# High parts of plain weight tiles written by rounding DMAs from HBM, without raw tiles

## The chip, the cores and the metric

The kernel runs on one core of a Trainium2 chip. The metric is the device time of one execution in microseconds (us), taken as the median of several runs. Beside the times there is one profiled execution with a trace of every instruction and DMA.

## The reference

One step of a streaming encoder with one layer. A prompt of 512 tokens and a sample of 64 tokens (with states and caches from earlier chunks) pass through the same weights: a mixer (gated DeltaNet beside gated linear attention), cross-attention into 256 memory tokens, and a ConvFFN, each behind an RMSNorm and with a residual. All numbers are float32.

```
def _mixer(h, p, l, conv_prev, s_a, s_b):
    proj = h @ p['w_in'][l]
    qkv, b_raw, a_raw, z_a, q_b, k_b, v_b, g_lr, z_b, gt_a, gt_b = _split_cols(proj, IN_SIZES)
    ...
    merged = jax.nn.sigmoid(gt_a) * y_a + jax.nn.sigmoid(gt_b) * y_b
    return merged @ p['w_o'][l], conv_new, s_a_new, s_b_new

def _conv_ffn(h, w_up, conv_w, conv_b, w_down, prev):
    u, new = _causal_dwconv(h @ w_up, conv_w, prev)
    u = u + conv_b
    gate, val = u[..., :D_FF], u[..., D_FF:]
    return (jax.nn.silu(gate) * val) @ w_down, new

def _trunk(...):
    x = x + _mixer(_rmsnorm(x, ...), ...)
    x = x + _cross_attn(_rmsnorm(x, ...), mem_k, mem_v, w_mq, w_mo)
    x = x + _conv_ffn(_rmsnorm(x, ...), w_up, conv_f_w, conv_f_b, w_down, ffn_prev)
    ...
    return _rmsnorm(x, norm_final), states
```

Outputs are the 576 rows of y, the new states of both attention kinds and both convolutions, and the memory keys and values.

## The kernel before

Tokens lie along the free axis (512 + 64 = 576 columns, in two halves of 288 or 290), channels on the 128 partitions. A weight tile is 128 x 1024: eight blocks of 128 x 128, which a projection (`proj`, `tile_proj`) multiplies with the eight chunks of x into one output chunk in PSUM (`sm`).

TensorE takes float32r operands, so every float32 operand is split in two: a rounded high part h and a low part lo = w - h. A product is then three matmuls: h with the high part of x, h with its low part, lo with its high part. For most weights (the kinds in `SUMMED`, line 177) the projection runs `late`: all matmuls with h first, two thirds of its time, then those with lo. Names in the trace: `w` are split weight tiles, h and lo alike; `wr` raw ones; `xh`, `xl`, `ach`, `acl` split activations; `gt` the mixer's gates; `fu`, `fc`, `fst`, `fout` the tiles of the FFN's convolution; `ws` sums of weights; `wt` and `wd` the weights in HBM, `wd` those of the down-projection, in pieces of 640 to 1024 columns that belong to parts of the 22 FFN chunks.

How a plain weight is made (`emit_weight`, lines 621 to 651): SyncE (SP) issues a load of the raw tile, float32, from HBM. ACT then writes lo = -raw with an ACTIVATE and h = raw with a CAST (`split_summed`). Then GpSimd (POOL) issues an accumulating DMA that reads the same weights from HBM again and adds them to lo. The few weights outside `SUMMED` (mk, mv and one tile of the down-projection) get lo by a subtraction of raw and h on DVE or POOL instead. A second kind of weights, marked "*" in the list `WORDER`, comes in pairs: seven products of sums of their halves take the place of eight (`emit_product`, line 660). They begin in the mixer's output projection and need raw tiles, from which DVE adds the sums `ws`.

Tiles live in rings: `w` with 6 tiles (WB), `raw` with 4 (RAWB), and in the FFN, where the mixer's space is free, 3 more `w` tiles (`wf`) and 1 more raw tile (`rawf`). `w_tile` and `raw_tile` take a tile whose last reader is done first (`Driver.first`). `fetch` (line 733) makes weights ahead in the order of `WORDER` as long as split tiles are left (`room`). From the up-projection on (`LATE0`), the split isn't made at once but some 25 us of the plan ahead of its use (`LEADD`, `defer`).

The first three weights come in halves between the chunks of x at the start (lines 765 to 776): SP alternates x, half a weight, x, half a weight.

All work passes through `Driver` (lines 251 to 509), which replays the program against a table of costs and puts every operation of ACT, DVE, POOL and SP at the place in its engine's order where it would come by the plan. Each engine runs its own instructions strictly in that order and waits at each for its inputs, and so an instruction that waits holds up all behind it. Every recorded operation has the line of the driver's helper, 292, so the views go by tile names.

Of the kernel before, what the change touches and what calls it, by code (L numbers as in the profile page):

```python
# [10 lines left out]
F32 = mybir.dt.float32  # L11
F32R = mybir.dt.float32r
I32 = mybir.dt.int32
AF = mybir.ActivationFunctionType
# [3 lines left out]
P = 128  # L18
D = 1024
# [6 lines left out]
SLOT = 582  # L26
HT = T // 2
NS = 59
RAWB = 4
NBANK = 8  # L30
SPARE = 2
OGO = ("oa", 3)
WB = 6
WF = 3
RF = 1
# [32 lines left out]
def weight_order():  # L68
    seq = list(HEADS)
    for m in range(NPG):  # L70
        seq += [("gta", m), ("gtb", m)]
    seq += [("*", u) for u in product_order(GPAIRS[:NG1], True)]
    seq += [("outb", m) for m in range(NB)]
    seq += [("outa", m) for m in range(NB)] + [("out", m) for m in range(NB, 4)]
    seq += [("*", u) for u in product_order(GPAIRS[NG1:])]
    seq += [("out", m) for m in range(max(NB, 4), 8)]
    for kd, i in ATT:
        if kd == "wo":
            seq += [("*", u) for u in product_order(WPAIRS, True)]
        else:  # L80
            seq += [(kd, 2 * i + j) for j in range(2)]
    seq += [("mo", 0), ("mo", 1)] + [("*", u) for u in product_order(MPAIRS, True)]
    for kd, i in FFN:
        if kd == "up":
            seq += [("up", i), ("up", NJ + i)]
        elif kd == "upx":
            seq.append(("*", (up_pair(i[0]), i[1])))
        elif kd == "dn1":
            seq.append(("dn", i))
        elif kd == "dns":  # L90
            seq += [("*", u) for u in product_order(i)]
        else:
            seq += [("dn", (m, 3)) for m in i]
    return seq
# [3 lines left out]
PARTS = [list(range(0, 5)), list(range(5, 11)), list(range(11, 18)), list(range(18, 22))]  # L98
# [54 lines left out]
WORDER = weight_order()  # L153
# [17 lines left out]
    WPRE.append(WPRE[-1] + weight_cost(w_))  # L171
LEADD, LEADV = 25.0, 18.0
LATE0 = WORDER.index(("up", 0))

# [5 lines left out]
def free(ap):  # L182
    n = 1
    for d in ap.shape[1:]:
        n *= d
    return n
# [64 lines left out]
class Driver:  # L251
# [82 lines left out]
        self.fresh.add(n)  # L334
        return tile_

    def first(self, tag, bufs, other, n):

        free = [(self.swapped if t in ("rawf", "wf") else 0.0) if len(self.ring.get(t, ())) < k else self.free_at(t)[0] for t, k in ((tag, bufs), (other, n))]
        return free[0] < free[1]  # L340

    def idle(self, name, bank=False):
        w, r = (max([0.0] + list(log.get(name, {}).values())) for log in (self.wrote, self.seen))
# [51 lines left out]
    def accumulate(self, out, in_, issuer):  # L395

        issue = self.place("G", self.open([out], []), 1.0)
        cost = self.FIXED["D"] + 2 * free(out) * self.PACE["D"]
        end = self.place("D", issue + 2.0, cost) + cost + 1.0
        self.mark(self.wrote, end, [out])  # L400
        self.put(issue, [(issuer.dma_start, (out, in_), dict(accum_op=ALU.add))])

    def hold(self, fn, cost, args, kw):
        out, ins = args[0], args[1:]
        self.due(self.now)
        t = max(self.ready_at(*ins), self.latest(self.seen, out), self.latest(self.ringed, out)) + HOP
        self.now = max(self.now, t)
        self.put(self.now, [(fn, args, kw)])
        self.now += cost
        self.mark(self.seen, self.now, ins)  # L410
        self.mark(self.wrote, self.now, [out])
        self.last = max(self.last, self.now)
        self.flush(self.now - BACK)
# [99 lines left out]
def tile_trunk(ctx, tc, xT, memT, wt, wd, vec, cst, w0, wgate, st_gdn, st_conv, st_gla, st_ffn, ckT, cv,  # L513
               o_y, o_gdn_p, o_conv, o_gla_p, o_ffn, o_mk, o_mv, o_gdn_s, o_gla_s):
    nc = tc.nc
    drv = PE = Driver(nc.tensor, nc.sync)
    V, A, G = Engine(drv, "V", nc.vector), Engine(drv, "A", nc.scalar), Engine(drv, "G", nc.gpsimd)
    X = Either(V, G)

    DMA, DMO = drv.load, drv.store  # L520
# [4 lines left out]
    wp = ctx.enter_context(tc.tile_pool(name="wp", bufs=2))  # L525
# [5 lines left out]
    fp = None  # L531

    def nm(s):
        cnt[0] += 1
        return f"{s}{cnt[0]}"
# [39 lines left out]
    def f(ap):  # L575
        return ap.bitcast(F32)
# [5 lines left out]
    def keep(t_):  # L582
        drv.pending.add(t_[:].tensor.name)
        return t_

    def drop(*aps):
        for ap in aps:
            drv.pending.discard((ap if hasattr(ap, "tensor") else ap[:]).tensor.name)

    def raw_tile():  # L590
        while all(n in drv.pending for tag in ("raw", "rawf") for n in drv.ring.get(tag, ())) and len(drv.ring.get("raw", ())) == RAWB:
            make(next(iter(unmade)))
        if fp is not None and drv.first("rawf", RF, "raw", RAWB):
            return keep(drv.rotate("rawf", RF, fp.tile([P, 1024], F32, tag="rawf", name=nm("wr"), bufs=RF)))
        return keep(drv.rotate("raw", RAWB, wp.tile([P, 1024], F32, tag="raw", name=nm("wr"), bufs=RAWB)))

    wnames = set()

    def w_tile():
        if fp is not None and drv.first("wf", WF, "w", WB):  # L600
            t_ = drv.rotate("wf", WF, fp.tile([P, 1024], F32R, tag="wf", name=nm("w"), bufs=WF))
        else:
            t_ = drv.rotate("w", WB, wp.tile([P, 1024], F32R, tag="w", name=nm("w"), bufs=WB))
        wnames.add(t_[:].tensor.name)
        return keep(t_)

    unmade = {}

    def make(i):
        fn = unmade.pop(i, None)  # L610
        if fn is not None:
            fn()

    def defer(i, fn, at):
        if i < LATE0:
            fn()
            return
        unmade[i] = fn
        drv.later(at, lambda: make(i))

    def emit_weight(i, at=0.0):
        kind, idx = WORDER[i]
        if kind == "*":
            wready[i] = emit_product(i, at, *idx)
            return
        raw = raw_tile()
        n = 1024
        if kind == "dn":
            m, p = idx
            n = len(PARTS[p]) * 128  # L630
            src = wd[m, :, PART0[p] * 128:PART0[p] * 128 + n]
        elif kind in ("outa", "outb"):
            n, c = 512, 512 * (kind == "outb")
            src = wt[WIDX[("out", idx)], :, c:c + 512]
        else:
            src = wt[WIDX[(kind, idx)]]
        DMA(raw[:, :n], src)
        h = w_tile()
        h, lo = (h[:, 0:512], h[:, 512:1024]) if n <= 512 else (h[:], w_tile()[:])
        summed = kind in SUMMED and (kind, idx) != ("dn", (7, 3))  # L640

        def split_():
            if summed:
                split_summed(h[:, :n], lo[:, :n], raw[:, :n], src)
            else:
                A.copy(h[:, :n], raw[:, :n])
                X.tensor_tensor(lo[:, :n], raw[:, :n], f(h[:, :n]), op=ALU.subtract)
            drop(raw[:])

        defer(i, split_, max(drv.ready_at(raw[:, :n]), at - (LEADD if summed else LEADV)))  # L650
        wready[i] = (h, lo)

    def split_summed(h, lo, raw, src):
        A.activation(lo, raw, AF.Copy, scale=-1.0)
        A.copy(h, raw)
        drv.accumulate(lo, src, nc.gpsimd)
# [3 lines left out]
    def emit_product(i, at, pair, prod):  # L660
# [32 lines left out]
        s1 = lambda: made("s1", lambda: a21, lambda: a22)  # L693
        s2 = lambda: made("s2", s1, lambda: a11)
        w = w_tile()
        h, lo = w[:, 0:n], w[:, 512:512 + n]
        summed = prod in ("P1", "P2", "Q4") or prod == "Q5" and n > 256 and pair[0][0] not in ("wo", "dn")
# [19 lines left out]
    def weight(kind, idx, ahead=True, held=False):  # L717

        i = wpos[0]
        assert WORDER[i] == (kind, idx), (WORDER[i], kind, idx)  # L720
        wpos[0] = i + 1
        for j in [j for j in wready if j < i - held]:
            drop(*wready.pop(j))
        if i not in wready:
            emit_weight(i)
        make(i)
        if ahead:
            fetch(i + 1, i)
        return wready[i]
# [3 lines left out]
    def fetch(i, now=None):  # L733

        now = i if now is None else now
        room = WB + (WF if fp is not None else 0)
        for j in range(i, len(WORDER)):
            if j in wready:
                continue
            if j >= wlimit[0]:  # L740
                break
            kd_, i_ = WORDER[j]
            if len(drv.pending & wnames) + (1 if kd_ in ("*", "outa", "outb") or kd_ == "dn" and len(PARTS[i_[1]]) <= 4 else 2) > room:
                break
            emit_weight(j, drv.now + WPRE[j] - WPRE[now])

# [15 lines left out]
    mbc_t = cp.tile([P, 256], F32, name="mbc")  # L762
    cst_t = small_tile([P, NM - 256], F32, tag="cst", name="cst", bufs=1)
    x = []
    raws = [wp.tile([P, 1024], F32, tag="raw", name=nm("wr"), bufs=RAWB) for _ in range(3)]
    for t_ in raws:
        keep(drv.rotate("raw", RAWB, t_))

    WPART = {k: (n // 2, 512 * (n % 2), 512 * (n % 2) + 512) for n, k in enumerate((0, 1, 2, 3, 5, 6))}
    for k in range(KT):  # L770
# [3 lines left out]
        if k in WPART:  # L774
            i, a, b = WPART[k]
# [294 lines left out]
    def c_heads():  # L1070

        while not drv.ready(OGO):
            yield WAIT
# [1544 lines left out]
```

## Time and profile before

| | |
|---|---|
| median of 3 runs | 1069.32 us (1068.57 to 1070.27) |
| span of the profiled execution | 1067.2 us |
| granted TensorE clock | 1.00 in all stretches |
| DMA packets | 171.33 MB, mean 161 GB/s |
| POOL `w <-` DMA issues waiting for ACT `w` | 407.2 us in 142 waits |
| ACT `w` waiting for PE `sm` (a tile not yet free) | 48.0 us in 43 waits |

The profiled execution is 2.1 us shorter than the median, which holds time outside the span as well. Rows of groups read: line, engine, operation, out<-in, shapes and count, then busy time, mean ns, and the idle time before with what ended it. Time that an engine other than TensorE sits idle costs nothing by itself.

### The profile page before, as it was taken

The numbers are of one execution on the slowest core, as the hardware profiler recorded it, in microseconds if no ns is written. First come the engines' busy times: TensorE is split into PE (matmuls) and PEld (weight loads), VectorE is DVE, ScalarE is ACT, GpSimd is POOL, SyncE is SP. The second block draws the span as 40 slices with busy tenths as digits, with TensorE's granted clock in tenths as the row PEclk, the third lists the DMA queues.
The fourth block names the chain that finished last, engine by engine and source line by source line (L and its number), as shares of the span: only waits on it lengthen the run. The fifth ranks groups of instructions, "written<-read, shape, count | busy, mean of one in ns | idle before, by whom it ended". The sixth has DMA issues, their size and how long they took to land.

```text
span 1067.2 us, 21405 instructions
## 1 busy us (share of the span) xinstructions
PE 1059.6 (99%) x8162; PEld 1045.0 (98%) x8162; DVE 749.7 (70%) x1480; ACT 704.6 (66%) x1410; POOL 356.5 (33%) x581
## 2 busy tenths in 40 slices
PE   9999999999999999999999999999999999999997
PEld 8999999999999999999999999999999999999997
DVE  6666855767675776878647676778877776688665
ACT  7665547555667667456666778767776775777645
POOL 1243216233534233124221235344343333332324
PEclk9999999999999999999999999999999999999999
DMA  9665345353449979588664467858887798878844
GB/s 303 147 142 138 64 121 128 76 123 85 123 76 209 214 162 264 192 226 221 175 165 139 81 166 180 194 111 176 183 191 168 155 218 188 185 159 190 183 90 111
DMA packets 68182, 171.33 MB, mean 161 GB/s; under 512 B 7920, under 2 KB 14576, under 8 KB 68080
## 3 DMA queue, kind: packets, MB, share of 16 engines
q0 software_dynamic: 30672, 71.19, 38.8%
q1 hardware_dynamic: 36976, 98.26, 28.1%
q8 instruction: 64, 1.05, 0.4%
q10 hardware_dynamic: 432, 0.53, 0.1%
q14 instruction: 38, 0.31, 0.1%
HBM read 157.50 MB, written 5.37 MB: 153 GB/s over the span
## 4 chain that ended last, share of the span: by engine, by line
PE 96%; DMA 1%; ACT 1%; issue 0%; DVE 0%; SPq 0%; ACTq 0%
PE sm L292 96%; DMA w<-wt 1%; ACT w L292 1%; DMA wr<-wt 0%; ACT gt L292 0%; DVE w L292 0%; DVE x L292 0%; DVE acl L292 0%; DVE yo L292 0%; ACT ao L292 0%; ACT ach L292 0%; ACT xh L292 0%; DVE xl L292 0%; SPq L292 0%; DVE ws L292 0%
## 5 line engine op out<-in xcount | busy, mean ns | idle before, releaser
L292 PE MATMUL sm<-xh,w 128*128 128x290 f32 (+3 forms) x2304 | 446.7, 300 | 0.2 <-DMA w<-wt 0.2
L292 PEld LDWEIGHTS sm<-xh,w 128*128 128x128 f32 x2304 | 356.7, 189 | 2.2 <-DMA w<-wt 0.4
L292 PE MATMUL sm<-xl,w 128*128 128x290 f32 (+3 forms) x1152 | 269.9, 295 | 0.2 <-DVE xl L292 0.2
L292 POOL DMA_DIRECT2D w<-wt x152 | 135.6, 904 | 339.7 <-ACT w L292 289.0
L292 PE MATMUL sm<-ach,w 128*128 128x288 f32 (+2 forms) x1212 | 231.0, 296 | 0.6 <-ACT gt L292 0.4
L292 PEld LDWEIGHTS sm<-xl,w 128*128 128x128 f32 x1152 | 200.4, 188 | 0.4 <-DVE xl L292 0.4
L292 PEld LDWEIGHTS sm<-ach,w 128*128 128x128 f32 x1212 | 189.7, 188 | 1.2 <-ACT gt L292 0.6
L292 ACT CAST w<-wr 128x512 fp32r<-128x512 f32 (+5 forms) x209 | 159.0, 764 | 18.9 <-PE sm L292 15.4
L292 ACT ACTIVATE w<-wr 128x512 fp32r<-128x512 f32 (+5 forms) x186 | 141.8, 764 | 23.3 <-PE sm L292 20.5
L292 PE MATMUL sm<-acl,w 128*128 128x256 f32 (+2 forms) x606 | 146.8, 295 | 0.2 <-DVE acl L292 0.2
L292 ACT CAST w<-ws 128x512 fp32r<-128x512 f32 (+1 forms) x136 | 80.3, 598 | 49.0 <-DVE ws L292 26.6
L292 PEld LDWEIGHTS sm<-acl,w 128*128 128x128 f32 x606 | 107.4, 188 | 0.5 <-DVE acl L292 0.5
L292 DVE TENSOR_TENSOR w<-ws,w 128x512 fp32r<-128x512 f32 (+1 forms) x108 | 73.5, 688 | 24.9 <-ACT w L292 22.9
L292 DVE SCALAR_TENSOR_TENSOR fc<-fu,vec,fc 128x578 f32<-128x578 f32 x88 | 70.5, 816 | 3.3 <-ACT fc L292 3.3
L292 PE MATMUL sm<-sh,w 128*128 128x290 f32 x288 | 61.2, 297 | 0.0
L292 DVE TENSOR_TENSOR x<-x,sm 128x320 f32<-128x320 f32 (+3 forms) x98 | 40.1, 437 | 22.9 <-PE sm L292 22.6
L292 POOL DMA_DIRECT2D w<-wd x34 | 29.8, 885 | 74.9 <-ACT w L292 65.1
L292 ACT ACTIVATE fc<-fu,vec 128x578 f32<-128x578 f32 x44 | 38.1, 871 | 15.1 <-POOL fu L292 14.8
L292 PEld LDWEIGHTS sm<-sh,w 128*128 128x128 f32 x288 | 47.6, 189 | 0.0
L292 DVE TENSOR_TENSOR ws<-ws,wr 128x512 f32<-128x512 f32 (+1 forms) x67 | 44.5, 664 | 1.1
L292 PE MATMUL sm<-oh,w 128*128 128x256 f32 (+1 forms) x256 | 45.1, 296 | 0.0
L292 PE MATMUL sm<-sl,w 128*128 128x290 f32 x144 | 39.8, 297 | 0.0
(401 smaller groups left out, 1933.4 us busy)
## 6 DMA issues: line engine op xcount, KB each, us to landing
wr<-wt SPq DMA_DIRECT2D x129, 512.0 KB, 5.7
w<-wt POOLq DMA_DIRECT2D x51, 512.0 KB, 7.0
w<-wt POOLq DMA_DIRECT2D x101, 256.0 KB, 6.3
w<-ws POOLq DMA_DIRECT2D x27, 256.0 KB, 5.3
x<-xT SPq DMA_DIRECT2D x16, 288.0 KB, 6.0
wr<-wt SPq DMA_DIRECT2D x14, 256.0 KB, 5.3
wr<-wd SPq DMA_DIRECT2D x8, 448.0 KB, 5.1
w<-wd POOLq DMA_DIRECT2D x8, 448.0 KB, 6.8
```

Source lines behind the costliest of these rows:

```text
L292: fn(*args, **kw)
```

## The change

For plain weights in `SUMMED` there is no raw tile any more. POOL issues a DMA from HBM straight into h, whose type is float32r, so the DMA rounds on its way (`Driver.cast`). ACT writes lo = -h from the rounded tile, and POOL's accumulating DMA adds the weights to it as before. The ACT cast and the SP load are gone. The products, mk, mv and the one tile of the down-projection are made as before. In the first stage, up to four weights before the first product (`EARLY`), the four raw tiles serve as further split tiles: `w_tile(both)` may take them and `fetch` counts them as room, so ten tiles are there instead of six. Which ring a tile comes from is decided by `Driver.sooner`, over as many rings as are offered.

```diff
+EARLY = next(i for i, w in enumerate(WORDER) if w[0] == "*") - 4
+RINGS = dict(w=WB, wf=WF, raw=RAWB, rawf=RF)
...
+    def cast(self, out, in_, issuer):
+
+        issue = self.place("G", self.open([out], []), 1.0)
+        cost = self.FIXED["D"] + free(out) * self.PACE["D"]
+        end = self.place("D", issue + 2.0, cost) + cost + 1.0
+        self.mark(self.wrote, end, [out])
+        self.put(issue, [(issuer.dma_start, (out, in_), {})])
...
+    def w_tile(both=False):
+        t_ = ring_tile(F32R, "w", "wf", *(("raw",) if both else ()))
         wnames.add(t_[:].tensor.name)
...
-        raw = raw_tile()
...
-        DMA(raw[:, :n], src)
-        h = w_tile()
-        h, lo = (h[:, 0:512], h[:, 512:1024]) if n <= 512 else (h[:], w_tile()[:])
         summed = kind in SUMMED and (kind, idx) != ("dn", (7, 3))
+        raw = None if summed else raw_tile()
+        h = w_tile(i < EARLY)
+        h, lo = (h[:, 0:512], h[:, 512:1024]) if n <= 512 else (h[:], w_tile(i < EARLY)[:])
+        if summed:
+            drv.cast(h[:, :n], src, nc.gpsimd)
+        else:
+            DMA(raw[:, :n], src)
 
         def split_():
             if summed:
-                split_summed(h[:, :n], lo[:, :n], raw[:, :n], src)
+                A.activation(lo[:, :n], f(h[:, :n]), AF.Copy, scale=-1.0)
+                drv.accumulate(lo[:, :n], src, nc.gpsimd)
...
-            if len(drv.pending & wnames) + (1 if ...) > room:
+            if len(drv.pending & wnames) + (1 if ...) > room + (RAWB if j < EARLY else 0):
```

By the count of instructions, POOL issues 297 DMAs where it issued 213, SP has 162 rows where it had 246, and ACT 1169 rows where it had 1250. TensorE has 7326 rows in both, with the same matmuls; in the first stage they interleave a little differently.

POOL at the start of the program, before (`w_317<-wt` is an accumulate onto a low part; `rt` and `u` belong to the first norm and the convolution):

```order
8 L292 MEMSET mhalf 128x16
9 L292 DMA w_317<-wt 128x1024
10 L292 MEMSET rin_366 128x8
11 L292 DMA w_320<-wt 128x1024
12 L292 MEMSET u_321 128x3
13 L292 DMA w_326<-wt 128x1024
```

And now; `w_315`, `w_317`, `w_322`, `w_324` and `w_326` are high parts, `w_316`, `w_318` and `w_323` low ones:

```order
8 L294 MEMSET mhalf 128x16
9 L294 DMA w_315<-wt 128x1024
10 L294 DMA w_317<-wt 128x1024
11 L294 DMA w_322<-wt 128x1024
12 L294 DMA w_324<-wt 128x1024
13 L294 DMA w_326<-wt 128x1024
14 L294 MEMSET rin_367 128x8
15 L294 DMA w_316<-wt 128x1024
```

Five rounding DMAs stand ahead of the first accumulate. The first waits for nothing, the second for DVE (a raw tile of the start), the next three for TensorE. On SP the loads of these tiles, which stood behind the constants, are gone.

ACT in the mixer's gates before, at the place of 400 us in the profile (`w_5233`, `w_5271` low parts, `w_5232`, `w_5270` high ones):

```order
471 L292 COPY gt_5229<-sm_5212 128x288
472 L292 ACTIVATE w_5233<-wr_5231 128x1024
473 L292 CAST w_5232<-wr_5231 128x1024
474 L292 COPY gt_5230<-sm_5234 128x288
475 L292 ACTIVATE w_5271<-wr_5269 128x1024
476 L292 CAST w_5270<-wr_5269 128x1024
477 L292 ACTIVATE gt_5088<-gt_5088 128x576
478 L292 ACTIVATE gt_5087<-gt_5087 128x576
```

And now:

```order
437 L294 COPY gt_5155<-sm_5138 128x288
438 L294 ACTIVATE w_5158<-w_5157 128x1024
439 L294 COPY gt_5156<-sm_5159 128x288
440 L294 ACTIVATE gt_5013<-gt_5013 128x576
441 L294 ACTIVATE gt_5014<-gt_5014 128x576
442 L294 COPY gt_5155<-sm_5138 128x288
```

Of four weight operations between the gates' one is left.

POOL in the down-projection between the chunks of the FFN, before (640-wide pieces are the plain weights; `w_9897` and `w_9919` low parts):

```order
379 L292 COPY fu_9646<-fst 128x2
380 L292 COPY fout<-fu_9646 128x4
381 L292 MEMSET fu_9898 128x2
382 L292 DMA w_9897<-wd 128x640
383 L292 DMA w_9919<-wd 128x640
384 L292 MEMSET fu_9943 128x2
```

And now the corresponding place (`w_9773`, `w_9793` high parts, `w_9774`, `w_9794` low ones):

```order
440 L294 DMA w_9773<-wd 128x640
441 L294 DMA w_9793<-wd 128x640
442 L294 COPY fu_9526<-fst 128x2
443 L294 COPY fout<-fu_9526 128x4
444 L294 MEMSET fu_9775 128x2
445 L294 DMA w_9774<-wd 128x640
446 L294 DMA w_9794<-wd 128x640
447 L294 MEMSET fu_9819 128x2
```

The two rounding DMAs, each waiting for TensorE to be done with a tile, stand ahead of the copies of `fu`, and the accumulates behind them.

More of the change, by code (lines that the diff above doesn't have):

```diff
@@ L28 @@
 NS = 59
-RAWB = 4
 NBANK = 8
@@ L32 @@
 OGO = ("oa", 3)
+RAWB = 4
 WB = 6
@@ L335, in rotate, with sooner @@
         return tile_
-    def first(self, tag, bufs, other, n):
-        free = [(self.swapped if t in ("rawf", "wf") else 0.0) if len(self.ring.get(t, ())) < k else self.free_at(t)[0] for t, k in ((tag, bufs), (other, n))]
-        return free[0] < free[1]
+    def sooner(self, *rings):
+        return min(rings, key=lambda r: (self.swapped if r[0] in ("rawf", "wf") else 0.0) if len(self.ring.get(r[0], ())) < r[1] else self.free_at(r[0])[0])
     def idle(self, name, bank=False):
@@ L588, in drop, with ring_tile @@
             drv.pending.discard((ap if hasattr(ap, "tensor") else ap[:]).tensor.name)
+    wnames = set()
+    def ring_tile(dt, *tags):
+        tag, bufs, pool = drv.sooner(*((t, RINGS[t], fp if t in ("wf", "rawf") else wp) for t in tags if fp is not None or t in ("w", "raw")))
+        return keep(drv.rotate(tag, bufs, pool.tile([P, 1024], dt, tag=tag, name=nm("w" if dt == F32R else "wr"), bufs=bufs)))
     def raw_tile():
@@ L592, in raw_tile @@
             make(next(iter(unmade)))
[L593 to L603, printed above, removed]
+        return ring_tile(F32, "raw", "rawf")
+    def w_tile(both=False):
+        t_ = ring_tile(F32R, "w", "wf", *(("raw",) if both else ()))
         wnames.add(t_[:].tensor.name)
-        return keep(t_)
+        return t_
     unmade = {}
@@ L647, in split_ @@
                 X.tensor_tensor(lo[:, :n], raw[:, :n], f(h[:, :n]), op=ALU.subtract)
-            drop(raw[:])
-        defer(i, split_, max(drv.ready_at(raw[:, :n]), at - (LEADD if summed else LEADV)))
+                drop(raw[:])
+        defer(i, split_, max(drv.ready_at(h[:, :n] if summed else raw[:, :n]), at - (LEADD if summed else LEADV)))
         wready[i] = (h, lo)
@@ L742, in fetch @@
             kd_, i_ = WORDER[j]
-            if len(drv.pending & wnames) + (1 if kd_ in ("*", "outa", "outb") or kd_ == "dn" and len(PARTS[i_[1]]) <= 4 else 2) > room:
+            if len(drv.pending & wnames) + (1 if kd_ in ("*", "outa", "outb") or kd_ == "dn" and len(PARTS[i_[1]]) <= 4 else 2) > room + (RAWB if j < EARLY else 0):
                 break
@@ L764, in tile_trunk @@
     x = []
-    raws = [wp.tile([P, 1024], F32, tag="raw", name=nm("wr"), bufs=RAWB) for _ in range(3)]
-    for t_ in raws:
-        keep(drv.rotate("raw", RAWB, t_))
+    raws = [raw_tile() for _ in range(3)]
     WPART = {k: (n // 2, 512 * (n % 2), 512 * (n % 2) + 512) for n, k in enumerate((0, 1, 2, 3, 5, 6))}
```

## The prediction

> **What bounds the kernel now.** I read the engine totals first, then the chain that ended last, then what TensorE (PE) waited for. The totals and queues of the page:
>
> ```profile
> PE 1059.6 (99%) x8162; PEld 1045.0 (98%) x8162; DVE 749.7 (70%) x1480; ACT 704.6 (66%) x1410; POOL 356.5 (33%) x581
> q0 software_dynamic: 30672, 71.19, 38.8%
> q1 hardware_dynamic: 36976, 98.26, 28.1%
> PE 96%; DMA 1%; ACT 1%; issue 0%; DVE 0%; SPq 0%; ACTq 0%
> ```
>
> TensorE is busy 99% of the 1067.2 us span and is 96% of the chain. The chain in order of time shows how rarely it stops (start, length, what):
>
> ```profile
> 6.32 396.67 PE sm L292 x3175
> ...
> 652.24 11.10 DMA w<-wt
> 663.38 164.57 PE sm L292 x1226
> ```
>
> For the first 397 us nothing holds it up. Its waits (total, times, longest) are all there is to win:
>
> ```profile
> PE warm L292 <- POOL acc L292: 1.0, 1, 1.0
> PE sm L292 <- ACT gt L292: 0.4, 1, 0.4
> PE sm L292 <- DVE x L292: 0.3, 1, 0.3
> PE sm L292 <- DVE acl L292: 0.2, 1, 0.2
> PE sm L292 <- DVE xl L292: 0.2, 1, 0.2
> PE sm L292 <- DMA w<-wt: 0.2, 1, 0.2
> ```
>
> Behind the start that is 1.3 us. A late matmul costs more than its row, because the one before it is drawn up to its full length: at 663 us,
>
> ```profile
> 662.81 0.42 PE L292 MATMUL sm<-xl,w 128*128 128x290 f32 x2
> 663.38 1.87 PE L292 MATMUL sm<-xh,w 128*128 128x290 f32 x12 [0.15 <-DMA w<-wt]
> ```
>
> at a pitch of 164.57/1226 = 0.134 us the next start was due at 662.81 + 2 x 0.134 = 663.08; it came 0.30 later, twice the 0.15 in the row. Doubling 1.3 gives an estimated **ceiling on any gain of 2.7 us**, 0.25%. The measurement can tell about 0.2%, 2.1 us, from no change.
>
> **What goes and what comes.** The casts that go, all on ACT (busy us, mean ns):
>
> ```profile
> L292 ACT CAST w<-wr 128x1024 fp32r<-128x1024 f32 x67 | 69.8, 1044 | 17.9 <-PE sm L292 14.9 <-issue 2.7 <-ACT w L292 0.4
> L292 ACT CAST w<-wr 128x512 fp32r<-128x512 f32 x109 | 66.1, 609 | 0.4 <-DMA wr<-wt 0.2
> L292 ACT CAST w<-wr 128x896 fp32r<-128x896 f32 x8 | 7.4, 932 | 0.0
> L292 ACT CAST w<-wr 128x768 fp32r<-128x768 f32 x8 | 6.6, 826 | 0.0
> L292 ACT CAST w<-wr 128x640 fp32r<-128x640 f32 x8 | 5.8, 720 | 0.6 <-PE sm L292 0.6
> L292 POOL DMA_DIRECT2D w<-wt x152 | 135.6, 904 | 339.7 <-ACT w L292 289.0
> ```
>
> By the order 51, 9, 8, 8 and 8 of them go: 53.2 + 5.5 + 7.4 + 6.6 + 5.8 = 78.5 us of ACT. As many loads leave SP (246 rows to 162) and come to POOL: 84 x 0.90 = 76 us, POOL from 356 to 432 us, 40%. Neither engine is the bound, so both sums are worth nothing by themselves; PE's 8162 matmuls stay, and their new interleaving in the first stage costs nothing (300 and 295 ns a matmul in all the large groups of the page). What counts is the few places where a weight or an operand is late.
>
> **Gain at 407 us, -0.6 us.** ACT's timeline there:
>
> ```profile
> 403.62 1.06 ACT L292 ACTIVATE w<-wr 128x1024 fp32r<-128x1024 f32 x1 [0.63 <-ACT gt L292]
> 404.58 1.03 ACT L292 CAST w<-wr 128x1024 fp32r<-128x1024 f32 x1
> 405.52 1.25 ACT L292 ACTIVATE gt<-gt 128x576 f32<-128x576 f32 x2
> ```
>
> The gate `gt`, for which PE waited 0.4 us, stood behind a weight's 1.06 and 1.03 us. In the new order one ACTIVATE stands among these rows where four operations stood. The other four waits are left as they are: three hang on DVE, and the 11.10 us DMA issued at 652 is one of POOL's 213, which become 297.
>
> **Price of a rounding DMA.** The trace has none. The nearest rows (KB each, median us from issue to landing) are plain loads and accumulates of one size:
>
> ```profile
> wr<-wt SPq DMA_DIRECT2D x129, 512.0 KB, 5.7
> w<-wt POOLq DMA_DIRECT2D x51, 512.0 KB, 7.0
> wr<-wd SPq DMA_DIRECT2D x8, 320.0 KB, 6.1
> w<-wd POOLq DMA_DIRECT2D x8, 320.0 KB, 6.5
> ```
>
> So 5.7 to 7.0 us for 512 KB and 6.1 to 6.5 for 320 KB. In engine time q0 pays 38.8/71.19 = 0.55% a MB, q1 28.1/98.26 = 0.29%: an accumulate reads two streams, a rounding copy one, so I take the plain end (no extra load on the DMA engines) and keep the other: the 38.5 MB that move would then add 10% to the engines' share. A cast that lands earlier than a plain load is not excluded, but worth nothing where nothing waits. The Trainium skill ("DMA: Bandwidth & Descriptors", Anatomy of one DMA) fits 2.0 us + bytes/436e3 for a DMA of this path, an estimated 3.2 us at 512 KB; by it every chain below would be about 6 us shorter and no site late, the sum -0.4 us. The 7.0 us row is more than twice that, in a kernel whose queues are shared, so I go by the rows.
>
> **The start, +0.2 us.** POOL and SP at the start, and the use of the last input chunk:
>
> ```profile
> 2.75 0.11 POOL L292 MEMSET mhalf<- 128x16 f32 x1 [1.77 <-ACT mhalf L292]
> 21.05 1.05 POOL L292 DMA_DIRECT2D w<-wt  x1 [18.19 <-ACT w L292]
> 13.55 2.27 SPq L292 DMA_DIRECT2D wr<-wt  x4
> 6.91 0.62 ACT L292 CAST w<-wr 128x512 fp32r<-128x512 f32 x1 [0.23 <-DMA wr<-wt]
> 8.17 0.69 PE L292 MATMUL sm<-xh,w 128*128 128x256 f32 x4
> 14.32 0.78 ACT L292 ACTIVATE xh<-x,vec 128x576 fp32r<-128x576 f32 x1
> 22.46 0.69 PE L292 MATMUL sm<-xh,w 128*128 128x256 f32 x4
> 0.00:25.00 25.00, 23.80 (x155) 22.51 (x155) 17.46 (x29) 19.72 (x30) 2.72 (x11) 1.00 0.90 306
> ```
>
> Before, the next weights were loaded behind all inputs (13.55 us). Now POOL's first cast waits for nothing and goes out right behind the memset, at about 2.9 us, into engines that are 0.90 busy at 306 GB/s; 512 KB is 1.7 us of that rate. If loads that were issued earlier go first, only late chunks are moved by 1.7 us a cast, and the last one's half is ready at 15.1 for a use at 22.46: 7 us of cover against two or three casts. If the cast shares evenly from its first packet, chunk 1, which ACT rounds at 7.53 for a use at 8.17, has 0.6 us of cover against up to 1.2. I take mostly the first, +0.2.
>
> **First stage, 0.** Ten tiles hold five weights of some 48 matmuls, 6 us each (396.67/3175 x 48); a pair of slots is free about four weights, 24 us, ahead of the low part's use. The new chain is cast 7.0 + ACTIVATE 1.06 + accumulate 7.0 + about 1 of waits, 16 us at the dear end. It fits.
>
> **Later stages, +1.4 us.** There the slots are nine, raw tiles serve the products, and the chain no longer starts before a slot is free: before, the raw tile was loaded ahead and slot-free to low part was ACT and one accumulate; now the cast comes on top, 4 to 7 us more. By the order 112 to 114 matmuls lie between the last read of a tile (w_9554, w_10037, w_4946) and the first use of the low part that needs its slot (w_9774, w_10254, w_5158): at 0.134 us, 15.0 to 15.3 us. The chain at 320 KB, with ACT's row for 128x640:
>
> ```profile
> L292 ACT ACTIVATE w<-wr 128x640 fp32r<-128x640 f32 x8 | 5.9, 741 | 1.8 <-PE sm L292 1.8
> 760.00:900.00 140.00, 139.99 (x1048) 139.70 (x1047) 103.16 (x175) 98.78 (x177) 51.13 (x97) 1.00 0.81 181
> ```
>
> 6.1 to 6.5 + 0.74 + 6.5 + 0.5 to 1.5 of waits on ACT and POOL = 13.8 to 15.2 us. At 512 KB: 5.7 to 7.0 + 1.06 + 7.0 + 0.5 = 14.3 to 15.6. Medians just fit; one in four late by 0.7 us is my estimate, and I count eight places with a lead of 15 to 17.5 us: 8 x 0.25 x 0.7 = 1.4. Behind a cast that waits for PE on POOL stand copies of `fu`, for which ACT already waits:
>
> ```profile
> ACT fc L292 <- POOL fu L292: 14.8, 17, 2.9
> ```
>
> I cost that at nothing: ACT has 41 us of the 140 free above, and PE never waited for `fc`. If that cover is gone, the 2.9 us row is the price of one place.
>
> **Sum:** -0.6 + 0.2 + 0 + 1.4 = +1.0 on the profiled 1067.2 us, which lies 2.1 below the median 1069.32 (time outside the span); so **1070.3 us**.
>
> **Rivals.**
> - **The longer chain decides (the slower side).** Misses at the thin leads are the rule: they begin when cast and accumulate together pass 13.5 us, where the medians give 12.6 to 14.0 and the DMA engines are 0.81 busy. Half a us to one at eight places: +4 to +6, about 1074. Against it: these medians contain the queueing of a mean place, and the two DMAs of one chain don't queue behind each other. Chance 0.28.
> - **Even sharing at the start.** Chunks 1 to 3 late by 0.6 at the plain price, up to 2.5 at an accumulate's: 1072.5. Chance 0.09.
> - **ACT's relief removes stalls and nothing new comes.** Up to -2.7: 1067. For it, the `gt` wait hangs on ACT, and those for `acl` and `xl` on DVE behind ACT's high parts; against it, 663 us hangs on a DMA of POOL's. Chance 0.08.
> - **The descriptors are held up by DVE.** A chain then has two such DMAs. POOL's issue would be stretched while DVE works; at 21.05 us, inside DVE's sums, it took 1.05 against a mean of 0.904, so at most 0.15 a DMA, 0.3 a chain. Were it 0.4 a DMA, eight places give 8 x 0.8 = 6: 1076. Chance 0.02. The Trainium skill ("SBUF — State Buffer", SBUF: two separate sides) warns of this: GpSimd can't write descriptors while DVE holds the shared port in a two-port mode; the 1.05 us row shows hardly any of it.
>
> **Chances.** Forecast 0.53, chain 0.28, start 0.09, relief 0.08, descriptors 0.02. The forecast's own range is -1.5 to +2.5. Faster by over 0.2%: 0.06 (most of the relief). Slower by over 0.2%: 0.28 + 0.05 + 0.02 + 0.03 = 0.38. Within: 0.56. The range leaves out the lower half of the relief and the upper part of the chain: 1067.4 to 1075.0.
>
> **What would show it.** Right: ACT about 626 us busy, POOL about 432, no wait of PE on ACT `gt` at 407, q0 near 110 MB, PE without a gap from 6 to 300 us, and short waits of PE on DMA w between 760 and 980 us where the 640-wide tiles of `wd` are first used. A rounding DMA that takes much over 6 us to land, or one that doubles q0's price a MB, makes the chain rival right; waits before 12 us the start's. No wait on DMA at all past 400 us would show that I took medians for what single transfers need.

## The result

| | before | changed |
|---|---|---|
| median | 1069.43 us (1068.57 to 1070.27) | 1082.95 us (1078.86 to 1084.62) |
| span of the profiled execution | 1067.2 us | 1077.1 us |

The ratio is 1.0122 (95% interval 1.0102 to 1.0143): 13.5 us slower, beyond the range of 1067.4 to 1075.0. The profiled execution, 1078.86 us, is the fastest of four; the other three have spans of 1080.5 to 1082.9 us at a mean granted clock of 0.996 to 0.998 for its 0.999, which the last section comes back to. The trace accounts for 9.9 us.

The changed kernel's page, totals and queues:

```profile
PE 1064.0 (99%) x8162; PEld 1046.5 (97%) x8162; DVE 753.6 (70%) x1481; ACT 635.6 (59%) x1326; POOL 406.3 (38%) x664
q0 software_dynamic: 42768, 109.73, 51.0%
q1 hardware_dynamic: 24880, 59.72, 17.1%
```

ACT gave up 69 us and POOL took 50 on; neither shows in the time, as forecast. TensorE's waits now (total, times, longest):

```profile
PE sm L294 <- DVE ot L294: 2.4, 2, 1.3
PE sm L294 <- ACT gt L294: 2.1, 1, 2.1
PE warm L294 <- POOL acc L294: 1.0, 1, 1.0
PE sm L294 <- DVE x L294: 1.0, 2, 0.6
PE sm L294 <- DVE ol L294: 0.5, 2, 0.3
PE sm L294 <- ACT oh L294: 0.4, 2, 0.2
```

Not one of them is on a DMA of weights. The chain in order of time says where they lie:

```profile
5.97 194.81 PE sm L294 x1562
...
277.94 3.43 issue
...
282.44 50.58 PE sm L294 x391
...
364.17 267.05 PE sm L294 x2042
...
659.73 389.97 PE sm L294 x2914
```

The start is as good as before (5.97 for 6.32 us). From 660 to 1050 us, in the FFN where I had put the misses, TensorE runs through without a stop. Nearly all is lost between 275 and 365 us: in matmuls done the changed kernel is 9 behind at 275 us, 74 at 365, and 72 at 660. The two kernels' work in the worst stretch (columns: window, length, busy us and count of PE, PEld, DVE, ACT, POOL, clock, DMA share, GB/s), before first:

```profile
330.00:365.00 35.00, 35.00 (x263) 33.81 (x262) 24.27 (x51) 23.03 (x47) 11.23 (x16) 1.00 0.94 216
```

```profile
330.00:365.00 35.00, 30.88 (x220) 27.76 (x219) 16.48 (x40) 15.95 (x36) 14.34 (x22) 1.00 0.83 176
```

43 matmuls fewer in 35 us; at 0.133 us each that is 5.7 us. How such a hole looks from inside: the timelines of TensorE, POOL and ACT of the changed kernel (start, length, engine, operation, and in brackets the idle time before with what ended it).

```profile
356.65 0.46 PE L294 MATMUL sm<-keep,ot 64*128 64x64 f32 x4 [1.15 <-DVE ot L294]
349.97 0.55 POOL L294 DMA_DIRECT2D w<-wt  x1 [1.63 <-PE sm L294]
353.15 0.55 POOL L294 DMA_DIRECT2D w<-wt  x1 [2.63 <-PE sm L294]
353.73 0.49 POOL L294 TENSOR_TENSOR ss<-ss,rr 64x4 f32<-64x4 f32 x2
356.81 0.63 ACT L294 ACTIVATE w<-w 128x512 fp32r<-128x512 f32 x1 [6.28 <-DMA w<-wt]
359.94 0.63 ACT L294 ACTIVATE w<-w 128x512 fp32r<-128x512 f32 x1 [2.50 <-DMA w<-wt]
360.48 1.23 ACT L294 CAST oh<-og 128x576 fp32r<-128x576 f32 x2
```

Three things come together. A rounding DMA waits on POOL for TensorE to free a tile (2.63 us), and the norm `ss`, on which `ot` hangs, stands behind it; ACT had its input ready at 350.5 us. On ACT the low part's ACTIVATE waits 6.28 and 2.50 us for rounding DMAs to land, and the casts of `oh` stand behind these. And TensorE, which before had projections left to fill such waits, has none here: it stops for `ot`.

### The profile page after: what moved, and what is told of

It reads as the page before. It is cut to its first block, busy times and chain, and to the rows that moved or that the text cites. A ratio compares the mean times of both kernels' runs of the same rounds, so it can differ in the third digit from the quotient of the medians.

```text
span 1077.1 us, 21341 instructions
## 1 busy us (share of the span) xinstructions
PE 1064.0 (99%) x8162; PEld 1046.5 (97%) x8162; DVE 753.6 (70%) x1481; ACT 635.6 (59%) x1326; POOL 406.3 (38%) x664
## 3 DMA queue, kind: packets, MB, share of 16 engines
q0 software_dynamic: 42768, 109.73, 51.0%
## 4 chain that ended last, share of the span: by engine, by line
PE 96%; DMA 1%; DVE 1%; ACT 1%; issue 1%; SPq 0%; POOL 0%; ACTq 0%; DVEq 0%; POOLq 0%
PE sm L294 95%; DMA wr<-wt 1%; PE warm L294 0%; SPq L294 0%; DMA w<-wt 0%; ACT w L294 0%; ACT oh L294 0%; DVE x L294 0%; DVE st L294 0%; DVE os L294 0%; DVE ot L294 0%; DVE ws L294 0%; DVE acl L294 0%; DVE ol L294 0%; DVE yo L294 0%
## 5 line engine op out<-in xcount | busy, mean ns | idle before, releaser
L294 POOL DMA_DIRECT2D w<-wt x211 | 170.7, 842 | 373.9 <-ACT w L294 228.0
L294 ACT ACTIVATE w<-w 128x1024 fp32r<-128x1024 f32 (+4 forms) x84 | 79.5, 950 | 64.1 <-DMA w<-wt 34.9
L294 ACT CAST w<-wr 128x512 fp32r<-128x512 f32 (+2 forms) x125 | 80.8, 649 | 11.0 <-PE sm L294 7.2
L294 POOL DMA_DIRECT2D w<-wd x59 | 45.2, 783 | 89.2 <-ACT w L294 44.6
L294 ACT ACTIVATE w<-wr 128x512 fp32r<-128x512 f32 (+1 forms) x102 | 61.9, 609 | 16.1 <-PE sm L294 13.4
```

The source lines that it names most:

```text
L294: fn(*args, **kw)
```

## The experiments

Three theories at first: **in-order** (what waits for a cast holds up others on POOL and ACT), **order** (the shared tiles change the first stage's interleaving; the first expectations call it the first-stage rival), **DMA** (a rounding DMA costs more than a load). A fourth, **chain** (the weights are late because the cast can start only in a free split tile), came after the first seven runs. The expectations call rounding DMAs casts.

Most kernels restrict where a weight is made by a rounding DMA; the rest is made from raw tiles as before:

```diff
+        casted = summed and (CONDITION)
-        raw = None if summed else raw_tile()
+        raw = None if casted else raw_tile()
...
-        if summed:
+        if casted:
             drv.cast(h[:, :n], src, nc.gpsimd)
...
-            if summed:
+            if casted:
...
+            elif summed:
+                split_summed(h[:, :n], lo[:, :n], raw[:, :n], src)
+                drop(raw[:])
```

"Not shared" stands for `EARLY = 0`; `EARLY0` then keeps the old number for conditions.

**e1: the FFN alone, not shared.** `i >= LATE0`.

> Rounding DMAs in the FFN alone, raw tiles everywhere before it, no shared tiles. In-order theory: nothing lost before 640 us, the FFN's gain of about 1.3 us kept, 0 to 1 us lost near 1050: 1067.5 to 1070. First-stage rival: the same. DMA rival: 32 of 84 casts, 1074.

1069.20 us, 1.0001 (0.9992 to 1.0011). The DMA rival's 1074 falls; the 32 casts of the FFN and its longer chains cost nothing.

**e2: the first stage alone, shared.** `i < EARLY`.

> Rounding DMAs and shared tiles in the first stage alone; raw tiles from the gates on. In-order theory: only the 277 us wait and small losses before 240 stay, 1072 to 1074. First-stage rival: 1080 or more. DMA rival: 21 to 24 of 84 casts, 1072.

1076.86 us, 1.0075 (1.0059 to 1.0092): +7.8. Above what the in-order theory allowed and below the first-stage rival's 1080. All the weights between are made from raw tiles here, and still TensorE stops near 356 us:

```profile
356.59 0.46 PE L294 MATMUL sm<-keep,ot 64*128 64x64 f32 x4 [1.43 <-DVE ot L294]
358.13 0.39 PE L294 MATMUL sm<-oh,w 128*128 128x256 f32 x1 [1.08 <-ACT oh L294]
```

**e5: all but the weights between, shared.** `i < EARLY or i >= LATE0`.

> Rounding DMAs in the first stage (with the shared raw tiles) and in the FFN; the 26 or so plain weights between (gates, output projections, query and memory output) made from raw tiles as before. In-order theory (PE loses where an ACTIVATE that waits for a cast's landing, or a cast that waits for PE, stands on ACT or POOL ahead of other work, between 240 and 365 us): the 335 and 355 to 364 us waits go, the 277 us one stays: 1071 to 1074. First-stage rival (the new interleaving by the shared tiles does it, wherever the casts are): still 1079 to 1083. DMA rival (casts cost more engine time than loads): loss in proportion to the casts left, 60 of 84, 1078.

1076.50 us, 1.0070 (1.0055 to 1.0085): as e2, so the FFN adds nothing here either. The in-order theory's 1071 to 1074 is missed.

**e4: the change, its split planned later.**

```diff
-        end = self.place("D", issue + 2.0, cost) + cost + 1.0
+        end = self.place("D", issue + 2.0, cost) + cost + 4.0
```

> The change as it is, but the planner takes a rounding DMA to land 3 us later, so that ACT's ACTIVATE and the accumulate stand later in their engines' order. In-order theory: ACT waits less at the head, the waits at 335 and 355 to 364 shrink, 1073 to 1079. First-stage rival and DMA rival: no change, 1079 to 1085.

1092.78 us, 1.0229 (1.0205 to 1.0254): 10 us worse. Moving the ACTIVATE back in ACT's order does not relieve TensorE, it makes the low parts late. In e4 TensorE waits for weights' DMAs, all of them issues of 0.87 to 0.92 us as accumulates are:

```profile
PE sm L294 <- DMA w<-wd: 5.8, 6, 1.4
PE sm L294 <- DMA w<-wt: 4.7, 2, 2.7
```

So a later place in ACT's order is no cure: the chain from cast to low part has no such room to give. That ACT's waiting is no part of the cause this doesn't show, since the edit moves the whole plan.

**e7: the DMAs alone.** The kernel before, with its raw tiles; the orders of TensorE, ACT and DVE are the same row for row.

```diff
-        DMA(raw[:, :n], src)
+        if kind in SUMMED and (kind, idx) != ("dn", (7, 3)):
+            drv.load(raw[:, :n].bitcast(F32R), src, nc.gpsimd)
+        else:
+            DMA(raw[:, :n], src)
```

> The kernel before with its raw tiles, its ACT casts and its orders on TensorE, ACT and DVE row for row; only the 86 raw loads of plain weights are issued by POOL as rounding DMAs into the raw tile. This is the price of the DMAs alone, with their places in POOL's order, and without slots becoming scarce. In-order theory: the raw tiles are free early, so few of them wait on POOL: 1069 to 1072. Order theory (the plan's new interleaving in the first stage and at its end does it): 1069. DMA rival (a rounding DMA costs much more than a load, or crowds the start): 1075 or more.

1070.69 us, 1.0015 (1.0006 to 1.0025). The same 42768 packets on q0 as in the change cost 1.5 us when they are prefetched into raw tiles. (POOL's count grew by 84, not 86.) The rounding DMAs of 512 KB landed within the 5.7 to 7.0 us that the prediction took:

```profile
wr<-wt POOLq DMA_DIRECT2D x51, 512.0 KB, 6.2
```

The DMA rival is out.

**e8: the first stage alone, not shared.** `i < EARLY0`.

> Rounding DMAs in the first stage alone as in e2, but the raw tiles aren't shared: six split tiles there. Order theory: without the four more tiles the weights come no earlier than before and the interleaving is near that of before, so the loss of e2 (7.8 us) mostly goes, 1069 to 1073. In-order theory: slots are scarcer, casts wait longer for TensorE on POOL and ACTIVATEs longer for casts on ACT: slower than e2, 1080 or more.

1071.00 us, 1.0016 (1.0007 to 1.0026). 5.9 us less than e2 with its ten tiles: more room made it slower. The in-order theory, which wanted 1080 or more, falls for this stage.

**e3: the whole change, not shared.**

> The whole change without the shared tiles (six split tiles in the first stage). Order theory: faster than the change, about 1075 (what the middle stage loses stays). In-order theory: as e8 against e2, slower than the change's 1083.

1080.18 us, 1.0102 (1.0087 to 1.0117), between the two forecasts. Against e8 the weights between and the FFN add 9.2 us, and e1 says it isn't the FFN. Here TensorE does wait for a weight:

```profile
345.30 0.63 ACT L294 ACTIVATE w<-w 128x512 fp32r<-128x512 f32 x1 [5.98 <-DMA w<-wt]
346.24 3.93 POOL L294 DMA_DIRECT2D w<-wt  x6 [3.77 <-ACT w L294]
356.75 0.63 ACT L294 ACTIVATE w<-w 128x512 fp32r<-128x512 f32 x1 [6.10 <-DMA w<-wt]
357.68 0.88 POOL L294 DMA_DIRECT2D w<-wt  x1 [7.52 <-ACT w L294]
361.86 1.57 PE L294 MATMUL sm<-oh,w 128*128 128x256 f32 x6 [2.71 <-DMA w<-wt]
```

These are e3's timelines of POOL, ACT and TensorE; its chain has from 347.60 us on

```profile
347.60 9.04 DMA w<-wt
```

ACT waits 5.98 us for earlier rounding DMAs, and POOL 3.77 us for ACT. Then POOL issues six DMAs in a row, two accumulates and four rounding DMAs; the first of these, issued at 347.60, takes 9.04 us to land; ACT makes the low part; the accumulate goes out at 357.68 and TensorE has waited 2.71 us when it lands near 361.8. From the issue at 347.60 to the use: 14.3 us.

**e9: the weights between alone, not shared.** `EARLY0 <= i < LATE0`.

> Rounding DMAs only between the first stage and the FFN (gates 0 and 1, output projections, mq, mo: 25 weights), no shared tiles, raw tiles elsewhere. Chain theory (there a cast can't start before a split tile is free, and two DMA trips are longer than the lead; the runs so far give e3 - e8 = 9.2 us for it): 1076 to 1079. Order theory (a disturbed first stage is what puts the middle out of step): below 1072.

1077.51 us, 1.0080 (1.0066 to 1.0094): +8.3 with the first stage made from raw tiles. The order theory's reading, that the middle only suffers from a disturbed first stage, falls. But the longest wait here is not one for a weight:

```profile
PE sm L295 <- DVE ot L295: 3.6, 1, 3.6
338.80 0.54 POOL L295 DMA_DIRECT2D w<-wt  x1 [2.36 <-PE sm L295]
340.39 0.53 POOL L295 DMA_DIRECT2D w<-wt  x1 [1.06 <-PE sm L295]
340.93 0.48 POOL L295 TENSOR_TENSOR ss<-ss,rr 64x4 f32<-64x4 f32 x2
```

Two rounding DMAs wait on POOL for TensorE, and `ss`, whose input ACT had ready at 336.3 us, starts behind them at 340.93; TensorE stops for `ot` until 343.94. That is the in-order theory's mechanism, in the middle stage. So the chain theory's forecast came true with more than its own mechanism at work.

**e11: as e3, but the output projections from raw tiles** (twelve weights; eight of them 256 KB, four 512 KB). `kind not in ("out", "outa", "outb")`.

> As e3 (rounding DMAs everywhere, no shared tiles), but the 256 KB weights of the output projections (out, outa, outb) are made from raw tiles. Chain theory: they are what is late between 345 and 420 us (in e3 a cast of theirs took 9.0 us to land behind five other DMAs of POOL's), so 1071 to 1073.5. If gates, mq and mo are late as well: 1075 or more.

1070.68 us, 1.0015 (1.0006 to 1.0025). Twelve of 84 weights carry 9.5 us of e3's loss. How much of it is late weights (e3's 2.71 us) and how much work held up behind waiting rounding DMAs (e9's 3.6 us on `ot`), no run separates: e11 takes both away. The stretch is whole again:

```profile
330.00:365.00 35.00, 35.00 (x266) 34.43 (x264) 19.62 (x40) 21.99 (x46) 12.91 (x19) 1.00 0.97 228
```

**e10: the change, raw tiles handed back sooner.** `- 10` for `- 4` in `EARLY`.

> The change with the raw tiles shared up to ten weights before the first product instead of four, so that they are free for the products sooner. If sharing costs because raw tiles come back too late: near e3, 1079 to 1081. If it costs because weights come early and TensorE spends its projections too soon: no better than the change, 1082 to 1085.

1081.97 us, 1.0120 (1.0106 to 1.0134): hardly better than the change, between the two forecasts. Its longest wait is a single one of 3.6 us for `ot`, as in e9, with two waiting rounding DMAs ahead of `ss` on POOL.

**e14: the change, output projections from raw tiles, shared as in the change.**

> The change, with the shared tiles as they are, but the output projections' 256 KB weights made from raw tiles. If the two costs are separate (chain of the output projections; shared tiles, under which the plan puts the sample's last solve and state update some 10 us later, rs at 340 us for 331), only the second stays, as in e2 and e5: 1075 to 1077.5, with rs at 338 us or later and TensorE waiting for ot and oh near 356. If the chain were the only cost: 1070 to 1072.

1077.73 us, 1.0085 (1.0068 to 1.0102). The second cost stays: with the outputs made from raw tiles, sharing takes 7.2 us (8.7 of e14 less 1.5 of e11). The state update of the sample's last solve, DVE's `rs` (min/median/max ns, first and last start), in the kernel before, in e11 and in e14:

```profile
L292 DVE SCALAR_TENSOR_TENSOR rs<-sm,sg,vb x4: 334/335/338, 329.6 to 331.1; 64x128 f32<-64x128 f32 x4
```

```profile
L295 DVE SCALAR_TENSOR_TENSOR rs<-sm,sg,vb x4: 331/332/334, 319.4 to 320.2; 64x128 f32<-64x128 f32 x4
```

```profile
L294 DVE SCALAR_TENSOR_TENSOR rs<-sm,sg,vb x4: 334/334/344, 340.8 to 341.6; 64x128 f32<-64x128 f32 x4
```

Under the shared tiles this serial chain stands 11 us later than before, and when it ends near 357 us there are no projections left to run beside it. The load of the sample's state (`sgd`) also goes out later, but in the changed kernel it has landed at 328.3 us, 10 us ahead of its first use, so it isn't what holds the chain there.

**e13: as e14, raw tiles handed back sooner.**

> As e14, with the raw tiles shared only up to ten weights before the first product. In e10 that brought rs back to 329 us. If the late sample chain is what sharing costs: 1070 to 1072.5, no wait for ot or oh near 350. If sharing costs by anything else, such as late raw tiles: 1075 or more.

1073.64 us, 1.0044 (1.0029 to 1.0059), between the two forecasts. `rs` is back at 328.2 us and the wait at 356 is gone, as expected, but a wait of 1.6 us for `xi` has come near 197 us. So handing the raw tiles back sooner takes off 4.1 of the 7.2 us that sharing costs, and the sample's chain comes back with it. That the chain's place is the cause is the likely reading, but not shown: the edit moves both, and raw tiles that come back too late for the products would go the same way. Of the 3.1 us that are left, the waits near 197 and 210 us (`xi` 1.6, `yc` 0.6) are 2.2.

**e12: the FFN without its last tile, not shared.** `i >= LATE0 and (kind, idx) != ("dn", (6, 3))`.

> As e1 (rounding DMAs in the FFN alone), but the last tile of the down-projection is made from a raw tile. e1 gained 0.3 us up to 1040 us and lost 0.9 after it; if the last tile's longer chain was that loss, 1068.3 to 1069, a fraction under the kernel before; if not, 1069 to 1069.5.

1068.56 us, 0.9994 (0.9985 to 1.0003). The best of all, 0.6 us under e1 and within the forecast, and not to be told from the kernel before.

The two causes in one table (loss in us against the kernel before in the same runs):

| | output projections by rounding DMA | from raw tiles |
|---|---|---|
| raw tiles shared | 13.5 (the change) | 8.7 (e14) |
| not shared | 11.0 (e3) | 1.5 (e11) |

They don't add up, 9.5 + 7.2 + 1.5 being 18.2: both leave TensorE without work in the same stretch, so one wait can cover another. That is the likely reason; no run shows it.

## Why the prediction was wrong

**What bounds the kernel: right. ACT's and POOL's sums: too large, which cost nothing.** No engine's relief was worth anything. ACT gave up 69 us for 78.5; rows of ACT that follow each other overlap by some 0.10 us (403.62 + 1.06 against 404.58 in the prediction's rows), an estimated 8 us over 84 casts. POOL grew by 50 us for 76: an issue of a rounding DMA that went out alone took 0.55 us in the rows above, where an accumulate has a mean of 0.90.

**Price of a rounding DMA: right.** q0's share grew by 12.2 points for 38.5 MB more, 0.32% a MB against a plain load's 0.29 and an accumulate's 0.55. The plain end held.

**The start, +0.2: near.** Nothing was lost there; the chain's first piece starts 0.35 us sooner.

**Gain at 407 us, -0.6: right in place.** Near 400 us the wait on `gt` is gone; in the changed kernel it sits at 335 us and is larger, 2.1 us: there ACT's copy of `gt` stands behind two weights, the first a split of a raw tile that had waited 3.05 us for TensorE.

**Later stages, +1.4: right mechanism, wrong place and size.** The step that failed is the chain's sum out of medians of single DMAs with 0.5 to 1.5 us of waits on ACT and POOL, at eight places chosen by their lead alone. In the FFN, where no weight was late, the 320 KB DMAs, casts and accumulates together, landed sooner than I took them; those of 384 KB, which by the same sum make a chain of 14.8 us, fitted too:

```profile
w<-wd POOLq DMA_DIRECT2D x16, 384.0 KB, 6.5
w<-wd POOLq DMA_DIRECT2D x16, 320.0 KB, 4.9
```

At 320 KB that is 2 x 4.9 + 0.74 + 1 = 11.5 us against a lead of 15.3. At the output projections the DMAs go out in one row: 9.04 us for a cast alone, and before the row POOL had waited 3.77 us for ACT and ACT 5.98 us for casts. From the cast's issue to the use it was 14.3 us, about my sum; what I had at 0.5 to 1.5 us were the waits ahead of the issue. My eight places ended at a lead of 17.5 us; the chain was late where DMAs are bunched, not where the lead is shortest. The casts of the output projections cost 9.5 us (e3 against e11), in late weights and in work held up behind them.

**First stage, 0: wrong.** The failed sentence is that the new interleaving "costs nothing (300 and 295 ns a matmul)". It looked at what a matmul costs and not at what the order leaves for later. TensorE's work with weights from 25 to 125 us, before and changed (window, length, busy us and count, clock, DMA share, GB/s):

```profile
25.00:125.00 100.00, 80.30 (x585) 1.00 0.58 129
```

```profile
25.00:125.00 100.00, 83.84 (x620) 1.00 0.70 148
```

With ten tiles the weights come sooner, and 35 projection matmuls more are done in this stretch, 3.5 us more of TensorE's time; the serial work of the heads is behind by as much. At the end of the stage the sample's chain comes after the projections instead of beside them. Sharing cost 5.9 us (e2 against e8) to 7.2 (e14 against e11). That the early projections are what makes the chain late isn't shown: in e13 as many are done as in the change,

```profile
25.00:125.00 100.00, 83.74 (x619) 1.00 0.68 143
```

and its chain is not late; e8, with 603, lost 1.8 us.

**POOL's work behind a waiting cast, cost at nothing:** right for `fu` in the FFN, wrong for `ss` before it, which the prediction did not look at (2.63 us of such a wait at 353 us, and e9's 3.6 us on `ot`). At 277 us in the changed kernel POOL's `gx`, behind a cast's wait of 2.23 us, came next to DVE's `ot`:

```profile
277.05 4.40 DVE L294 TENSOR_TENSOR ot<-ot,ss 128x512 f32<-128x512 f32 x2
277.45 0.62 POOL L294 DMA_DIRECT2D w<-wt  x1 [2.23 <-PE sm L294]
278.09 2.79 POOL L294 TENSOR_TENSOR gx<-xh,xl 128x576 f32<-128x576 f32 x2
```

Two such DVE operations took 4.40 us, where one has a median of 0.68, and TensorE waited 1.25 us for them. That `gx` or the DMA's issue beside it stretched `ot` is a guess from this one place; no run takes it apart.

**The chances.** The chain rival, given 0.28, named the right kind of mechanism and a price half of what came, but its thin leads in the FFN missed nothing; no rival held that more tiles can be worse. Of the signs, no wait on `gt` at 407 us and q0 at 110 MB came; TensorE without a gap up to 300 us did not (1.25 us at 281), nor did short waits in the FFN. And there was no wait on a DMA past 400 us, which was to show that I took medians for what single transfers need.

Open: by which of its choices the plan with shared tiles puts the sample's chain later, and the 1.5 to 1.8 us that rounding DMAs cost in e7, e8 and e11. In e7 a new wait of 0.9 us for an accumulate onto a sum's low part is the larger piece:

```profile
PE sm L292 <- DMA w<-ws: 0.9, 1, 0.9
```

## What to carry to other kernels

A staging buffer that looks superfluous may be what lets a load begin before its final place is free; taking it out saves the copy and puts the load's whole time, queueing included, behind the release of the tile, so look at every place where DMAs go out in a row, and at what stands behind each wait on the issuing engine. And in a kernel that is bound by TensorE, filler work is a stock: a new order can leave none for the last serial chain, so compare where the serial chains stand in it, not only how long each operation takes.

## What the runs showed of the hardware

**A short stop can cost twice.** TensorE in e2, by the microsecond:

```profile
355.00:357.00 2.00, 0.57 (x6) 0.33 (x4) 1.41 (x3) 0.00 (x0) 0.09 (x1) 1.00 1.07 298
357.00:359.00 2.00, 0.66 (x4) 0.37 (x3) 1.75 (x6) 1.59 (x3) 0.00 (x0) 1.00 0.97 233
360.00:361.00 1.00, 1.00 (x6) 0.89 (x6) 1.00 (x3) 0.85 (x2) 0.36 (x1) 0.58 0.00 0
361.00:362.00 1.00, 1.00 (x6) 1.00 (x5) 0.97 (x2) 0.44 (x1) 0.52 (x1) 0.50 0.52 98
362.00:363.00 1.00, 1.00 (x6) 1.00 (x5) 0.90 (x2) 1.00 (x3) 0.51 (x1) 0.50 1.08 203
363.00:364.00 1.00, 1.00 (x8) 1.00 (x7) 0.75 (x2) 0.84 (x3) 0.35 (x1) 0.72 0.99 178
```

In the 4 us up to 359 TensorE was busy for 1.23. Some 1.2 us after it was busy again the granted clock fell to 0.50 and stayed low for some 3.4 us, 0.42 + 0.50 + 0.50 + 0.28 = 1.7 us of work lost on top of the stop. The Trainium skill ("TensorE: Matmul & The Clock Gate", Part 1: The HAM clock gate) tells of half the clock after an idle window of about 3.4 us, and of the full clock again after a busy one of that length. The half clock and its length agree; but no single wait of TensorE here was longer than 1.43 us, so a stretch that is mostly idle was enough. In e14, 4 us with 2.16 us of work (357 to 361) left the clock at 1.00.

By the clock of their traces e2, e3, e5, e9 and e10 have one such fall each before their end and e4 three, every one 3.41 us long; the change, e13 and e14 have none in their profiled executions. All profiled executions fall to half once more at their end, so a mean clock of 0.998 alone tells of no loss. The three slower executions of the change, at 0.996 to 0.998 for 0.999, may hold such falls: 0.003 of 1080 us would be 3.2 of the 4.1 us between its profiled execution and its median. They have no trace, and the one at 0.998 (1083.62 us) was slower than one at 0.996 (1082.29 us), so the clock can't be all of it.

**The cost of issue and of landing part ways.** A rounding DMA holds POOL for a shorter time than an accumulate: in e7 84 of them added 46.6 us to POOL's busy time, 0.55 us each, for a mean of 0.90. It takes hardly more of the DMA engines than a plain load (0.32% a MB for 0.29). What it cost here came from where it had to wait.
